# A layer's second product on one core: its operands split where they are made, and stored as two words

## The chip, the core and the metric

The kernel runs on one core of a Trainium2 chip. A core has TensorE (PE in the profile, with PEld for its weight loads), VectorE (DVE), ScalarE (ACT), GpSimd (POOL) and SyncE (SP), each with its own queue of instructions, which it works off in order and in which a semaphore wait holds everything behind it. SP issues most DMAs here, ACT and POOL issue some. The metric is the device time of one execution in microseconds (us), the median of several; lower is better.

## The reference, cut to what matters

```python
x1 = ln(alpha * x + (1 + g1) * (merged @ w_out), ...)   # 1024 rows of the prompt and 64 of the sample, 1024 wide
u2 = x1 * (1 + sc2) + sh2
f  = square(relu(u2 @ w_up + b_up)) @ w_down + b_down    # 1024 -> 4096 -> 1024
y  = ln(alpha * x1 + (1 + g2) * f, ...)
```

The first two thirds of the time go to the recurrent and attention branches that make `merged`; the change does not touch them. It touches the last third: the **up stage** (`u2 @ w_up`, bias, relu, square) and the **down stage** (`... @ w_down`).

## The kernel before

All products are done with three matmuls in place of one (`mm3`, lines 110 to 113): each float32 operand is split into a high word, rounded to the format that TensorE multiplies, and a low word, the rest. ACT writes the high word (a Copy), DVE subtracts it from the source for the low word. Line 111 is high by high, 112 and 113 are the cross terms. Weights are split after each load by `wsplit` (lines 91 to 99: raw tile `wr`, words `wh` and `wl`, three buffers of each) or `split` (101 to 108).

The 1088 tokens stand as columns in three groups: 0 and 1 of 384 columns, 2 of 320. The hidden width of 4096 is 32 blocks of 128, worked in 16 **pairs** of two blocks.

**The up stage.** Pairs 0 and 1 are computed beside the end of the layer before (`up_mm`, tiles `up` and `hr`), pairs 2 and 3 plainly (`up`, `c`), pairs 4 to 15 in groups 0 and 1 by Strassen's scheme: seven products of half size, into three PSUM tiles `xu`, `zu`, `yu`, in the order x, z, x with the sum T2, y with T1, x with T3, y, x with T4. Between them `after` copies and adds the products on ACT and DVE to the four results `c0` to `c3`; a product that adds to `xu` waits for the copy that reads `xu` (`c_0` from ACT before T2, `c_1` before T3). The sums T1 to T4 are built once from u2 (lines 700 to 722, tiles `tt`). Group 2 is plain: tiles `ug`, results `cg`. `put_pair` (630 to 641) then forms four further sums `t` on POOL from the pair's four results, and writes seven 128 by 384 tiles to the scratch tensor `hs_d` in device memory, three by DMAs of ACT's queue, four by POOL's; `put_g2` writes group 2's results to `hg_d`.

**The down stage.** Group 2's product for hidden blocks of the first half comes first: sixteen blocks of 24 matmuls (`dg`), by weights `wr_dg` and operands `hg`; its accumulator `fg` is loaded from `facc_d`, scaled, and added to. Then Strassen chunks 0 to 3 (tiles `xd`, `zd`, `yd`): each chunk needs seven operands `op` from `hs_d` and adds to `facc`. After them group 2's second half, and the last normalization. Each operand is loaded raw (tag `opr`, two buffers) and split by `op_split` into `oph` and `opl` (seven buffers each). The loads are issued by SP in one order. The last pair's group 2 (pair 15, `ug15`) is done on the way over, its result in `cgl`.

The order of instructions on each engine is set when the program is built, by a scheduler that follows the dependences; `tc.issue_after` puts an instruction behind another one.

## Time and profile before

| | |
|---|---|
| median of three runs | 1742.97 us (1742.93 to 1744.25) |
| the profiled execution: its own time | 1744.55 us |
| the profiled execution: its span | 1742.8 us |
| PE busy | 1703.7 us, 98% of the span |
| DVE, ACT, POOL busy | 1008.6, 779.9 and 403.3 us |
| DMA, mean over the span | 125 GB/s |

The span is the profiled time from the first to the last instruction; some 1.7 us of the execution's own time lie around it. Busy shares are averages over stages with different limits; where an engine stood idle, and which instruction of another engine ended the idle time, is to be read stage by stage.

### The profile page before, as it was taken

What the parts mean: (1) busy time and instruction counts of PE and PEld (TensorE: products, weight loads), DVE (VectorE), ACT (ScalarE), POOL (GpSimd) and SP (SyncE); (2) the same over time, 40 slices, a digit from 0 to 9 for tenths busy, and PEclk for the clock granted to TensorE, in tenths of its full rate; (3) what the DMA queues carried; (4) which work ended last, traced back from release to release, by engine and by line L of the source; (5) the groups of instructions that cost most, each with busy time, mean ns of one, the idle gap of its engine ahead of it and who ended that gap; (6) DMA issues with size and microseconds to landing.
All of it is one profiled execution on the core that took longest, in us unless ns stands there. A gap on an engine that the chain in (4) does not pass through costs nothing.

```text
span 1742.8 us, 26601 instructions
## 1 busy us (share of the span) xinstructions
PE 1703.7 (98%) x10632; PEld 1668.7 (96%) x10632; DVE 1008.6 (58%) x1605; ACT 779.9 (45%) x1169; POOL 403.3 (23%) x408
## 2 busy tenths in 40 slices
PE   7999999999999999999999999999999899999996
PEld 4999999999999999999999999999999799999996
DVE  4586553745537455374656758233332477898876
ACT  2452443625435253352634445455554753344343
POOL 1100010000100001000013233556664134443323
PEclk8999999999999999999999999999999999999999
DMA  9242312223131221212246633333333773454443
GB/s 355 96 131 70 102 51 71 75 70 102 51 105 53 75 84 57 99 55 70 63 137 206 194 120 128 129 127 127 127 128 129 284 280 116 171 185 148 159 167 108
DMA packets 88044, 218.08 MB, mean 125 GB/s; under 512 B 11504, under 2 KB 42480, under 8 KB 87920
## 3 DMA queue, kind: packets, MB, share of 16 engines
q1 hardware_dynamic: 71936, 188.46, 32.0%
q10 hardware_dynamic: 11888, 15.34, 2.5%
q0 software_dynamic: 4096, 12.59, 2.0%
q8 instruction: 83, 1.36, 0.3%
q14 instruction: 41, 0.34, 0.1%
HBM read 171.53 MB, written 44.83 MB: 124 GB/s over the span
## 4 chain that ended last, share of the span: by engine, by line
PE 91%; DVE 3%; DMA 2%; issue 2%; ACT 2%; POOL 0%; SPq 0%; DVEq 0%; ACTq 0%; POOLq 0%
PE z L113 13%; PE z L112 13%; PE z L111 13%; PE po L408 3%; PE s L397 2%; PE dg L111 2%; PE dg L113 2%; PE xd L111 2%; PE dg L112 2%; PE xd L113 2%; PE xd L112 2%; PE xu L111 2%; PE xu L112 2%; PE xu L113 2%; PE op L113 2%
## 5 line engine op out<-in xcount | busy, mean ns | idle before, releaser
L111 PE MATMUL z<-uh,wh_in 128*128 128x384 f32 (+1 forms) x1320 | 436.6, 331 | 2.9 <-ACT uh L103 2.9
L112 PE MATMUL z<-ul,wh_in 128*128 128x384 f32 (+1 forms) x1320 | 437.0, 331 | 0.8 <-DVE ul L104 0.8
L113 PE MATMUL z<-uh,wl_in 128*128 128x384 f32 (+1 forms) x1320 | 436.0, 330 | 0.0
L111 PEld LDWEIGHTS z<-uh,wh_in 128*128 128x128 f32 x1320 | 248.7, 188 | 6.3 <-ACT uh L103 3.9
L112 PEld LDWEIGHTS z<-ul,wh_in 128*128 128x128 f32 x1320 | 248.6, 188 | 4.9 <-DVE ul L104 2.8
L113 PEld LDWEIGHTS z<-uh,wl_in 128*128 128x128 f32 x1320 | 248.6, 188 | 4.0 <-issue 3.1
L97 ACT ACTIVATE wh_in<-wr_in 128x1024 fp32r<-128x1024 f32 x56 | 59.4, 1060 | 96.3 <-PE z L112 91.4
L98 DVE TENSOR_TENSOR wl_in<-wr_in,wh_in 128x1024 fp32r<-128x1024 f32 x56 | 68.4, 1221 | 40.3 <-ACT wh_in L97 40.3
L113 PE MATMUL dg<-ophg,wl_dg 128*128 128x320 f32 x256 | 79.8, 313 | 4.8 <-DVE wl_dg L98 4.8
L111 PE MATMUL dg<-ophg,wh_dg 128*128 128x320 f32 x256 | 80.8, 316 | 3.1 <-ACT wh_dg L97 3.1
L112 PE MATMUL dg<-oplg,wh_dg 128*128 128x320 f32 x256 | 79.7, 311 | 0.0
L161 DVE SCALAR_TENSOR_TENSOR ap<-ar,sil,ap 128x512 f32<-128x512 f32 x112 | 79.7, 743 | 0.0
L380 ACT ACTIVATE pr<-pr,st 128x640 f32<-128x640 f32 (+2 forms) x64 | 44.7, 698 | 57.6 <-DVE st L379 57.4
L457 POOL MEMSET er<- 128x1 f32 x8 | 1.1, 135 | 297.1 <-DVE rt L453 297.1
L104 DVE TENSOR_TENSOR slo_u<-sr_u,shi_u 128x1024 fp32r<-128x1024 f32 x24 | 31.3, 1305 | 64.9 <-ACT shi_u L103 64.9
L104 DVE TENSOR_TENSOR wlo_u<-wr_u,whi_u 128x1024 fp32r<-128x1024 f32 x24 | 34.7, 1447 | 56.7 <-ACT whi_u L103 56.7
L104 DVE TENSOR_TENSOR opl<-op,oph 128x1536 fp32r<-128x1536 f32 x28 | 59.8, 2136 | 12.9 <-ACT oph L103 12.8
L363 DVE COPY v<-vt 128x512 f32<-128x512 f32 x16 | 11.1, 691 | 97.0 <-PE vt L362 97.0
L103 ACT ACTIVATE shi_d<-sr_d 128x1024 fp32r<-128x1024 f32 x32 | 33.8, 1057 | 74.2 <-PE yd L112 56.5
L404 ACT ACTIVATE pts<-pt 128x512 f32<-128x512 f32 (+2 forms) x64 | 33.2, 519 | 74.5 <-PE pt L402 73.5
L408 PE MATMUL po<-pts,v 128*128 128x128 f32 x480 | 64.1, 275 | 0.5 <-ACT pts L404 0.3
L408 PEld LDWEIGHTS po<-pts,v 128*128 128x128 f32 x480 | 61.2, 191 | 1.2 <-ACT pts L404 1.2
(384 smaller groups left out, 4581.1 us busy)
## 6 DMA issues: line engine op xcount, KB each, us to landing
wr_in<-in_w_in SPq DMA_DIRECT2D x56, 512.0 KB, 3.3
ar<-in_w_ada SPq DMA_DIRECT2D x46, 512.0 KB, 4.9
op<-hs_d SPq DMA_DIRECT2D x28, 768.0 KB, 4.9
wr_u<-in_w_up SPq DMA_DIRECT2D x33, 512.0 KB, 3.6
wr_dg<-in_w_down SPq DMA_DIRECT2D x32, 512.0 KB, 4.3
wr_d<-in_w_down SPq DMA_DIRECT2D x32, 512.0 KB, 4.0
wr_o<-in_w_out SPq DMA_DIRECT2D x24, 512.0 KB, 3.5
hs_d<-t POOLq DMA_DIRECT2D x64, 192.0 KB, 2.9
```

Source lines behind the costliest of these rows:

```text
L97: hlast[0] = S.activation(hi, raw, AF.Copy).ins
L98: V.tensor_tensor(lo, raw, hi.bitcast(F32), op=ALU.subtract)
L103: first = S.activation(hi, src, AF.Copy).ins
L104: V.tensor_tensor(lo, src, hi.bitcast(F32), op=ALU.subtract)
L111: TE.matmul(ps, wh, xh, start=first, stop=False, skip_group_check=more)
L112: TE.matmul(ps, wh, xl, start=False, stop=False, skip_group_check=more)
L113: TE.matmul(ps, wl, xh, start=False, stop=last, skip_group_check=more)
L161: V.scalar_tensor_tensor(part[:, w, :], raw[:, j, :], sil[:, kb, w:w + 1], part[:, w, :], op0=ALU.mult, op1=ALU.add)
L380: S.activation(pr[:rows, :W], pr[:rows, :W], AF.Exp, bias=st[:rows, 0:1], scale=-1.0, accum_out=st[:rows, 1:2])
L397: TE.matmul(sps[:, bk, :cw], qq[:, q0:q0 + P], kk[:, P * j0 + c0:P * j0 + c0 + cw], start=(ip == 0), stop=(ip == 2))
L404: S.activation(pts[:, :min(W, 512)], pt[:, :min(W, 512)], AF.Copy)
L408: TE.matmul(po[:, :P], v[:, j0 + j, :], pts[:, P * j:P * j + P], start=(j == 0), stop=(j == nk - 1))
```

## The change

Every tile that goes to `hs_d` or `hg_d` is now split where it is made, and both words are written: `halves_of` has ACT copy the source into the first half of a new tile `o` (pair and number, `o14_3`; `og` for group 2) and DVE subtract into the second, and the DMA carries both, 384 KB in place of 192 KB. From pair 2 on, the `o` tiles share the three buffers of tag `tt`, of which each is free again when its DMA has landed. In the down stage `op_split` is gone: SP loads `hg` and `op` straight into operand tiles with both words (1280 KB and 1536 KB in place of half), all from one set of eight buffers. The first weight of the down stage is loaded ahead of `hg`. The 16 instructions that scale `fg` are GpSimd's (line 878 of the changed kernel) and no longer ACT's (867).

```diff
-        hs_d = dp.tile([NFF // 8, 7, P, 4, GW], F32, name="hs_d")
-        hg_d = dp.tile([P, NFF, TW2], F32, name="hg_d")
+        hs_d = dp.tile([NFF // 8, 7, P, 4, 2, GW], F32, name="hs_d")
+        hg_d = dp.tile([P, NFF, 2, TW2], F32, name="hg_d")
...
+        onew = [lambda nm: big([P, 2, GW], nm)]
+
+        def new_o(nm):
+            return onew[0](nm)
+
+        def halves_of(src, nm, o=None):
+
+            if o is None:
+                o = new_o(nm)[:, :, 0:src.shape[-1]]
+            S.activation(o[:, 0, :].bitcast(R32), src, AF.Copy)
+            V.tensor_tensor(o[:, 1, :], src, o[:, 0, :], op=ALU.subtract)
+            return o
+
         def put_pair(p, c11, c12, c21, c22, g2s, new_t):
...
             for k, src in enumerate((c11, c21, t2, t1, t3, c22, t4)):
-                (S if k in (0, 1, 5) else G).dma_start(hs_d[c, k][:, i, :], src)
+                (S if k in (0, 1, 5) else G).dma_start(hs_d[c, k][:, i, :, :], halves_of(src, f"o{p}_{k}"))
...
-        def put_g2(p, b, src):
+        def put_g2(p, b, src, o=None):
             c, i = divmod(p, 4)
-            S.dma_start(hg_d[:, 8 * c + 4 * b + i, :], src)
+            S.dma_start(hg_d[:, 8 * c + 4 * b + i, :, :], halves_of(src, f"og{p}_{b}", o))
...
+        onew[0] = lambda nm: fp.tile([P, 2, GW], F32, tag="tt", bufs=3, name=nm)
+
         def up_g2(p, wa, wb):
...
-                c = cgs[b] if p == LATE else fp.tile([P, TW2], F32, tag="cg", bufs=2, name=f"cg{p}_{b}")
+                if p == LATE and b > 0:
+                    cgs.append(hp.tile([P, 2, TW2], F32, tag="cg", name=f"cgl{b}"))
+                c = cgs[b][:, 1, :] if p == LATE else fp.tile([P, TW2], F32, tag="cg", bufs=2, name=f"cg{p}_{b}")
                 relu2(c, ps[:, :TW2], f)
-                put_g2(p, b, c)
+                put_g2(p, b, c, cgs[b] if p == LATE else None)
...
-        cgs = [hp.tile([P, TW2], F32, tag="cg", bufs=2, name=f"cgl{b}") for b in range(2)]
+        cgs = [hp.tile([P, 2, TW2], F32, tag="cg", name="cgl0")]
         facc = {fb: new_facc(fb) for fb in range(4)}
-        hi_ins = []
-
-        def op_split(src, nm):
-            hl = [hp.tile(list(src.shape), R32, tag=t, bufs=7, name=f"{t}{nm}") for t in ("oph", "opl")]
-            hi_ins.append(split(*hl, src))
-            return hl
 
         def load_hg(c, h):
-            o = hp.tile([P, 4, TW2], F32, tag="opr", bufs=2, name=f"hg{c}_{h}")
-            loads.append(SY.dma_start(o, hg_d[:, 8 * c + 4 * h:8 * c + 4 * h + 4, :]).ins)
-            return op_split(o, f"g{c}_{h}")
+            o = hp.tile([P, 4, 2, TW2], R32, tag="op", bufs=8, name=f"hg{c}_{h}")
+            loads.append(SY.dma_start(o.bitcast(F32), hg_d[:, 8 * c + 4 * h:8 * c + 4 * h + 4, :, :]).ins)
+            return o[:, :, 0, :], o[:, :, 1, :]
...
-                                    S.activation(fg[:, fb, c0:c1], fg[:, fb, c0:c1], AF.Identity, scale=sA[:, fb:fb + 1],
-                                                 bias=bA[:, fb, w:w + 1])
+                                    G.tensor_scalar(fg[:, fb, c0:c1], fg[:, fb, c0:c1], sA[:, fb:fb + 1], bA[:, fb, w:w + 1],
+                                                    op0=ALU.mult, op1=ALU.add)
...
-        hg = {(0, h): load_hg(0, h) for h in range(2)}
-        with tc.issue_after(loads[1]):
-            pre = [wsplit(a["w_down"][0, 0], "dg0_0_0")]
-        with tc.issue_after(hi_ins[0]), tc.issue_after(hlast[0]):
+        pre = [wsplit(a["w_down"][0, 0], "dg0_0_0")]
+        with tc.issue_after(wlast[0]):
+            hg = {(0, h): load_hg(0, h) for h in range(2)}
+        with tc.issue_after(hlast[0]):
             up_g2(LATE, *wt)
...
-                o = hp.tile([P, 4, GW], F32, tag="opr", bufs=2, name=f"op{c}_{k}")
+                o = hp.tile([P, 4, 2, GW], R32, tag="op", bufs=8, name=f"op{c}_{k}")
                 with tc.issue_after(wloads[-1] if c == 0 and k > 4 else loads[-1]):
-                    loads.append(SY.dma_start(o, hs_d[c, k]).ins)
-                ops.append(op_split(o, f"{c}_{k}"))
+                    loads.append(SY.dma_start(o.bitcast(F32), hs_d[c, k]).ins)
+                ops.append((o[:, :, 0, :], o[:, :, 1, :]))
```

The built programs differ in order at three places that matter below. First DVE, where pairs 0 and 1 end (`uf`, `u2h`, `u2l`: the last columns of u2; `wl_u2` is the low word of pair 2's weights). Before:

```order
L586 TENSOR_SCALAR uf2_256_9692<-nT2_256_9690,s2_8188,b2_8189 128x64 x8
L104 TENSOR_TENSOR u2l2_9360<-uf2_256_9692,u2h2_9359 128x8x64
L98 TENSOR_TENSOR wl_u0_9815<-wr_u0_9812,wh_u0_9814 128x1024
L705 TENSOR_TENSOR tt0_0_9888<-u2h0_8527,u2l0_8528 128x768
L705 TENSOR_TENSOR tt0_1_9889<-u2h1_8939,u2l1_8940 128x768
L705 TENSOR_TENSOR tt0_2_9890<-u2h1_8939,u2l1_8940 128x768
L713 TENSOR_TENSOR tt0_0_9888<-tt0_1_9889,tt0_0_9888 128x768
L98 TENSOR_TENSOR wl_u2_9941<-wr_u2_9938,wh_u2_9940 128x1024
L98 TENSOR_TENSOR wl_u6_9947<-wr_u6_9944,wh_u6_9946 128x1024
```

and in the changed program, from the middle of pair 1's subtractions on (line 640; the subtractions of `o0_0` to `o0_3` stand ahead of `u2l`, the rest of pair 0 and `o1_0`, `o1_1` after it):

```order
L640 TENSOR_TENSOR o1_2_9905<-t1_1_9890,o1_2_9905 128x384
L640 TENSOR_TENSOR o1_3_9909<-t1_0_9889,o1_3_9909 128x384
L640 TENSOR_TENSOR o1_4_9913<-t1_2_9891,o1_4_9913 128x384
L640 TENSOR_TENSOR o1_5_9917<-hr5_9626,o1_5_9917 128x384
L640 TENSOR_TENSOR o1_6_9921<-t1_3_9892,o1_6_9921 128x384
L640 TENSOR_TENSOR og1_0_9925<-hr1_9523,og1_0_9925 128x320
L640 TENSOR_TENSOR og1_1_9929<-hr5_9626,og1_1_9929 128x320
L718 TENSOR_TENSOR tt0_0_9942<-u2h0_8527,u2l0_8528 128x768
L718 TENSOR_TENSOR tt0_1_9943<-u2h1_8939,u2l1_8940 128x768
L718 TENSOR_TENSOR tt0_2_9944<-u2h1_8939,u2l1_8940 128x768
L726 TENSOR_TENSOR tt0_0_9942<-tt0_1_9943,tt0_0_9942 128x768
L98 TENSOR_TENSOR wl_u2_9995<-wr_u2_9992,wh_u2_9994 128x1024
```

All of pairs 0 and 1 now stands ahead of the three joins, the subtraction and `wl_u2`; ACT's copies for them stand in the same order on ACT, the last nine (`o1_0` to `o1_6`, `og1`) and those of `og0` behind the square of `hr0`.

Second ACT, between pair 14 and pair 15 (lines 617 and 618 are relu and square; 802 and 807 of the kernel before are 819 and 824 of the changed one). Before:

```order
L618 ACTIVATE c14_2_12370<-c14_2_12370 128x384
L618 ACTIVATE cg14_1_12568<-cg14_1_12568 128x320
L639 DMA hs_d_87<-c14_2_12370 128x384
L645 DMA hg_d_88<-cg14_1_12568 128x320
L802 ACTIVATE c15_0_12572<-xu15_12602 128x384
L617 ACTIVATE c15_0_12572<-c15_0_12572,bup_78 128x384
L618 ACTIVATE c15_0_12572<-c15_0_12572 128x384
L639 DMA hs_d_87<-c15_0_12572 128x384
L807 ACTIVATE c15_1_12573<-xu15_12602 128x384
L809 ACTIVATE c15_3_12575<-yu15_12604 128x384
```

and now:

```order
L617 ACTIVATE c14_2_12748<-xu14_12776,bup_78 128x384
L618 ACTIVATE c14_2_12748<-c14_2_12748 128x384
L639 ACTIVATE o14_1_12889<-c14_2_12748 128x384
L639 ACTIVATE o14_2_12893<-t14_1_12878 128x384
L639 ACTIVATE o14_3_12897<-t14_0_12877 128x384
L819 ACTIVATE c15_0_12977<-xu15_13007 128x384
L652 DMA hs_d_87<-o14_1_12889 128x768
L617 ACTIVATE c15_0_12977<-c15_0_12977,bup_78 128x384
L618 ACTIVATE c15_0_12977<-c15_0_12977 128x384
L639 ACTIVATE o14_4_12901<-t14_2_12879 128x384
L639 ACTIVATE o14_5_12905<-c14_3_12749 128x384
L824 ACTIVATE c15_1_12978<-xu15_13007 128x384
```

Five copies (line 639) and other instructions stand between pair 14's last square and `c15_1`; `o14_4` waits for the landing of `o14_1`'s DMA and `o14_5` for that of `o14_2`'s, whose buffers they take. On PE in the changed program pair 15's x, z and y with T1 stand ahead of pair 14's last product, so that T2, T3 and T4 of pair 15 follow pair 14's T4 with no other matmul but pair 15's y between them; before, x, z and y of pair 15 stood between.

Third SP, at the start of the down stage (each row is one DMA). Before:

```order
L848 DMA hg1_0_12842<-hg_d_88 128x1280
L848 DMA hg1_1_12848<-hg_d_88 128x1280
L863 DMA fg_12807<-facc_d_86 128x8x320
L93 DMA wr_dg0_0_3_12909<-in_w_down 128x1024
L93 DMA wr_dg0_1_0_12939<-in_w_down 128x1024
L93 DMA wr_dg0_1_1_12987<-in_w_down 128x1024
L897 DMA op0_0_13361<-hs_d_87 128x1536
L905 DMA facc0_12729<-facc_d_86 128x768
L905 DMA facc1_12730<-facc_d_86 128x768
L897 DMA op0_1_13367<-hs_d_87 128x1536
L93 DMA wr_dg0_1_2_13019<-in_w_down 128x1024
L93 DMA wr_dg0_1_3_13051<-in_w_down 128x1024
```

and now, the same stretch, from the third `hg` on:

```order
L859 DMA hg1_0_13264<-hg_d_88 128x2560
L859 DMA hg1_1_13266<-hg_d_88 128x2560
L874 DMA fg_13229<-facc_d_86 128x8x320
L93 DMA wr_dg0_0_2_13293<-in_w_down 128x1024
L93 DMA wr_dg0_0_3_13323<-in_w_down 128x1024
L908 DMA op0_0_13775<-hs_d_87 128x3072
L908 DMA op0_1_13777<-hs_d_87 128x3072
L908 DMA op0_2_13779<-hs_d_87 128x3072
L908 DMA op0_3_13781<-hs_d_87 128x3072
L916 DMA facc0_13154<-facc_d_86 128x768
L916 DMA facc1_13155<-facc_d_86 128x768
L93 DMA wr_dg0_1_0_13353<-in_w_down 128x1024
```

Four whole `op` tiles and two `facc` now stand ahead of `wr_dg0_1_0`, the weights of the fifth of the sixteen blocks `dg`, where one row `op` stood behind three of the rows `wr_dg`.

## Rows read from the trace of the kernel before

**Rows 1.** The page: the chain that ended last, by engine.
```profile
PE 91%; DVE 3%; DMA 2%; issue 2%; ACT 2%; POOL 0%; SPq 0%; DVEq 0%; ACTq 0%; POOLq 0%
```

**Rows 2.** Timeline of PE, 1036 to 1056 us: start, length, instruction, [idle before].
```profile
1037.57 0.71 PE L111 MATMUL up<-u2h,wh_u 128*128 128x320 f32 x3 [1.68 <-ACT u2h L103]
...
1054.72 0.34 PE L113 MATMUL up<-u2h,wl_u 128*128 128x384 f32 x1
```

**Rows 3.** Timeline of DVE, 1036 to 1049 us.
```profile
1037.55 0.69 DVE L104 TENSOR_TENSOR u2l<-uf,u2h 128x512 fp32r<-128x512 f32 x1 [0.70 <-ACT u2h L103]
...
1044.06 2.69 DVE L705 TENSOR_TENSOR tt<-u2h,u2l 128x768 f32<-128x768 f32 x3
...
1047.54 1.22 DVE L98 TENSOR_TENSOR wl_u<-wr_u,wh_u 128x1024 fp32r<-128x1024 f32 x1
```

**Rows 4.** Timeline of ACT, 1034 to 1056 us (ACTq: a DMA issue).
```profile
1053.60 0.47 ACT L618 ACTIVATE hr<-hr 128x320 f32<-128x320 f32 x1
1054.10 0.33 ACTq L645 DMA_DIRECT2D hg_d<-hr  x1
```

**Rows 5.** ACT's groups by form, 1100 to 1350 us: busy us, mean ns, idle before.
```profile
L618 ACT ACTIVATE c<-c 128x384 f32<-128x384 f32 x45 | 23.6, 524 | 1.1
...
L617 ACT ACTIVATE c<-c,bup 128x384 f32<-128x384 f32 x35 | 21.4, 612 | 50.8 <-DVE c L811 31.9 <-DVE c L804 18.9
...
L807 ACT ACTIVATE c<-xu 128x384 f32<-128x384 f32 x12 | 5.7, 472 | 2.4 <-DMA hg<-hg_d 2.4
```

**Rows 6.** One of DVE's groups by form, 1100 to 1350 us.
```profile
L811 DVE TENSOR_TENSOR c<-xu,c 128x384 f32<-128x384 f32 x12 | 6.7, 557 | 23.4 <-PE xu L113 23.4
```

**Rows 7.** Two of POOL's groups by form, 1100 to 1350 us.
```profile
L639 POOL DMA_DIRECT2D hs_d<-t x47 | 25.8, 551 | 0.0
...
L637 POOL TENSOR_TENSOR t<-c,t 128x384 f32<-128x384 f32 x12 | 12.3, 1027 | 0.2
```

**Rows 8.** DMA issues, 1200 to 1300 us: KB each, median us from issue to landing.
```profile
wr_u<-in_w_up SPq DMA_DIRECT2D x10, 512.0 KB, 3.5
hs_d<-t POOLq DMA_DIRECT2D x17, 192.0 KB, 3.4
hs_d<-c ACTq DMA_DIRECT2D x14, 192.0 KB, 1.9
```

**Rows 9.** Stretches: length, busy (count) of PE, PEld, DVE, ACT, POOL, clock, DMA share, GB/s.
```profile
1170.00:1191.30 21.30, 21.30 (x131) 21.30 (x131) 7.06 (x7) 11.11 (x20) 12.56 (x13) 1.00 0.37 126
1366.00:1368.00 2.00, 2.00 (x9) 2.00 (x9) 2.00 (x3) 0.00 (x0) 0.00 (x0) 0.50 0.86 323
1370.00:1380.00 10.00, 7.46 (x51) 7.20 (x50) 1.38 (x1) 7.49 (x17) 0.00 (x0) 1.00 1.04 421
1480.00:1500.00 20.00, 19.33 (x111) 19.01 (x111) 17.33 (x16) 10.43 (x10) 9.03 (x4) 1.00 0.56 199
1500.00:1520.00 20.00, 20.00 (x117) 19.86 (x116) 15.62 (x20) 5.29 (x6) 10.37 (x8) 1.00 0.43 165
1600.00:1620.00 20.00, 18.76 (x106) 17.93 (x105) 17.55 (x17) 10.38 (x9) 7.56 (x4) 1.00 0.73 249
```

**Rows 10.** Timeline of PE at the first matmul of pair 15's T3.
```profile
1346.74 0.44 PE L111 MATMUL xu<-T3h,shi_u 128*128 128x384 f32 x1 [0.63 <-ACT c L807]
```

**Rows 11.** Timeline of PE from the end of the up stage to the first chunk.
```profile
1353.12 0.31 PE L111 MATMUL ug<-u2h,whi_u 128*128 128x320 f32 x1
...
1360.15 0.31 PE L111 MATMUL dg<-ophg,wh_dg 128*128 128x320 f32 x1
...
1365.39 0.58 PE L113 MATMUL dg<-ophg,wl_dg 128*128 128x320 f32 x1 [4.78 <-DVE wl_dg L98]
...
1380.21 0.42 PE L111 MATMUL dg<-ophg,wh_dg 128*128 128x320 f32 x1 [2.75 <-ACT wh_dg L97]
...
1426.74 0.34 PE L111 MATMUL xd<-oph,whi_d 128*128 128x384 f32 x1
```

**Rows 12.** DMA issues, 1366 to 1376 us.
```profile
wr_dg<-in_w_down SPq DMA_DIRECT2D x2, 512.0 KB, 8.7
```

More of the change, by code (lines that the diff above doesn't have):

```diff
@@ L951, in final2_open @@
                     TE.transpose(pt[:cw, P * fb:P * fb + P], fg[:, fb, c:c + cw], ident)
-                y = hp.tile([P, D], F32, tag="shi" if c < 2 * P else "opl", bufs=2 if c < 2 * P else 7, name=f"y2_{c}")
+                y = hp.tile([P, D], F32, tag="shi" if c < 2 * P else "op", bufs=2 if c < 2 * P else 8, name=f"y2_{c}")
                 S.activation(y[:cw, halves[0]], pt[:cw, :], AF.Copy)
```

## The prediction

> **What bounds the kernel now.** I read the chain that ended last first: 91% of it is PE [rows 1], so time is gained or lost only where PE waits. Then the stretches of the last third. A stretch as long as one pair of the up stage shows PE busy without a gap, with ACT at 11.1 of 21.3 us and DVE at 7.1 [rows 9]: both have room, if what they do comes in time. Last the few places where PE stands idle: 1.68 us before the last columns of u2 [rows 2], 0.63 us in pair 15 [rows 10], and the start of the down stage [rows 11]. There 48 matmuls `ug` take 7.03 us from 1353.12 to 1360.15, so 0.1465 each; the sixteen blocks `dg` of 24 should take 56.3 us, and the first chunk should begin at 1416.4. It begins at 1426.74: 10.3 us are lost, 4.78 and 2.75 of them in two waits, the rest in short ones and in a clock that stood at 0.50 behind the first [rows 9]. At that clock 13 matmuls cost about 1.6 us more than at the full one; behind the 2.75 us the clock was 1.00. In the chunks a stretch holds 117 matmuls where nothing is lost, and 111 to 106 in the three in which a chunk gives way to the next [rows 9].
>
> **Pairs 0 and 1.** The change adds, for each pair, nine copies on ACT and nine subtractions on DVE. A copy is as `c_1`'s, 0.47 us; a subtraction as line 811's, 0.56 us [rows 5, 6]; DMA issues are 0.33 us on ACT [rows 4]. What counts is where they stand. Four subtractions stand ahead of `u2l`'s last part, for which PE waits within a microsecond [rows 2, 3]: 2.2 us less the 0.7 us that DVE idles there, **+1.5 us**. Then, as the order shows, eleven copies and four DMA issues follow the square of `hr0`, which ends at 1054.07 [rows 4]: 11 x 0.47 + 4 x 0.33 = 6.5, to 1060.6. DVE's last subtraction ends at 1061.2; only then come the joins and the subtraction that before ran from 1044.06 to 1047.54, 3.5 us, and `wl_u2`, 1.22 us [rows 3]: 1065.9. PE uses `wl_u2` at 1054.72 [rows 2], with nothing else to do, as its queue holds the matmuls in order. **+11.2 us**, and +1.6 for the clock, since a wait of 4.78 us was enough to halve it. The later sums T then have the time that PE was given: nothing.
>
> **Steady pairs.** ACT gets 4.2 us and DVE 5.0 us per pair, which fits the room above. But a tile `o` takes one of three buffers, free when its DMA has landed. A tile of 384 KB was not timed; 192 KB took 1.9 us from ACT's queue and 3.4 from POOL's, 512 KB 3.5 from SP's [rows 8]. I take 2.5 and 3.5, nearer to the small ones, since most of a landing does not grow with size between these rows. Nine tiles in three rounds of some 5 us fit the pair of 21.3 us. In pairs 4 to 13 the scheduler has the next pair's products as filler before T3; by the same reckoning as below `c_1` is there at about the same time as PE, and I take **+2 us** for ten pairs (0 to 5). POOL's added waits before its next weight sums are covered by a whole pair.
>
> **Pairs 14 and 15.** There the filler ends. Pair 14: T3 follows T2 by two matmuls, and ACT's `c14_1` stands behind three copies of pair 13, of which the first waits for a DMA issued some 3 us earlier: **+2.6 us**. Pair 15, counted from A, the end of pair 14's T4: relu 0.6, square 0.5, three copies 1.4, `c15_0` 0.5 [rows 5]: T2 starts at A+3.0 and not at A. `o14_1`'s DMA is issued at A+3.3 and lands at A+5.8; `o14_2`'s is issued on POOL behind `t14_3` (1.03) and 0.55 of issue [rows 7], and lands at A+6.4; two copies, then `c15_1` at A+7.4, where T2 was done at A+5.1. T3 and y take 4.1 us, to A+11.5; the addition on DVE that T4 needs stands behind `og14_1`, whose buffer chain ends in the landing of `o14_4` at A+11.1, so A+13.1. Lost 3.0 + 2.3 + 1.6 = 6.9, before 0.63 [rows 10]: **+6.3 us**.
>
> **The start of the down stage.** Let E be the end of pair 15's T4 (before, 1353.12). Gained: no splits of `hg`, and GpSimd scales `fg`, so that ACT is free for `wh_dg`, which 2.75 us were lost to. Lost: the weights. In the order of SP's queue, what is still to be moved from about E+4 until `wr_dg0_1_0` has landed is three `hg` (3.9 MB), `fg` 1.3, four `wr_dg` 2.1, four `op` 6.3, two `facc` 0.8: 14.4 MB. The engines of the DMAs were full (share 1.04) at 421 GB/s [rows 9]; at 0.41 MB a us that is 35 us. A weight load in such a stretch landed 8.7 us after its issue, against 3.5 in the calm [rows 8, 12]: transfers queued on SP come behind those queued before. So the weight lands at E+39 + 2 = E+41 if pair 15's written tiles (3.3 MB, in other queues) are gone by then, and at E+49 if they take their full share: I take E+44.5, and 2.3 us for the two words. PE needs it after `ug` and four blocks, 7.0 + 14.1 = E+21.1, so it will have lost 25.7 us, before it 10.3: **+15.4 us** (12 to 20), and +1 for a clock that falls again. What follows comes 1.3 us apart, faster than PE's 3.5 us blocks.
>
> The Trainium skill, "DMA: Bandwidth & Descriptors" (Specifications), gives about 358 GB/s as what device memory yields to one core; by it, 14.4 MB would take 40 us, and this term would be 5 us more. The trace's 421 GB/s disagrees, and the trace decides.
>
> **The chunks.** ACT and DVE lose 28 splits of `op`; PE lost 6 matmuls of 20/117 = 0.171 us at the first of the three transitions and 11 at the last, 1.0 and 1.9 us, so 4 to 5 us in all. Eight buffers are free one after the other, a load of 1.5 MB takes 4 us, and PE needs them about 4 us apart: I take **-4 us** (0 to -5).
>
> **The sum.** 1.5 + 11.2 + 1.6 + 2 + 2.6 + 6.3 + 15.4 + 1 - 4 = +37.6. The profiled execution took 1744.55 us, 1.6 above the median of the runs: 1744.55 + 37.6 - 1.6 = 1780.5, **1780 us**.
>
> **Rivals.**
> Weights overtake: if SP's transfers share the engines and do not queue, `wr_dg0_1_0` lands some 10 us after its issue and PE waits there as before or less: without the 16.4 us, 1764 us. For it: transfers were spread over 16 engines; against it [rows 12].
> The Trainium skill, "DMA: Bandwidth & Descriptors" (Queues, rings and completion order), says that completion is not first-in first-out for one issuing engine, though descriptors start in ring order; that speaks for a part of this rival. The landing of 8.7 us [rows 12] disagrees with it where one queue is full, and so the rival has 0.14 and no more.
> ACT bounds the steady pairs: if a landing takes 5 us and not 2.5 to 3.5, `c_1` comes 2 us late in ten pairs, +18 more: 1798 us. It decides from a landing of about 4 us; [rows 8] speak against it for ACT's queue, less for POOL's.
> Faster: DVE reaches `wl_u2` before 1054.72, because the copies of pairs 0 and 1 fall into idle time of ACT, and with every operand ready as it lands the down stage loses nothing. Then -10.3 - 4.5 + 1.5 + 8.9 + 2 = -2.4, and with half of the two last pairs' waits -6.9: 1736 us. It decides at the start of the joins, which must be before 1050. Against it stands the built order, with eleven copies behind the square of `hr0`.
> No change: the losses above halve and the gains come in full: 1744 us.
>
> **Chances.** Forecast 0.60 (1768 to 1794), weights overtake 0.14, ACT bound 0.12, faster 0.09, no change 0.05. What a measurement can tell from no change is about 0.2%, 3.5 us. Range 1757 to 1802: it takes in both rivals beside the forecast and leaves out the last two and the tails. Faster 0.09, same 0.05, slower 0.86.
>
> **What would show it.** PE waiting some 11 us for DVE's `wl_u` at line 98, near 1056 us; PE waiting for ACT's `c` (lines 819, 824) twice at the end of the up stage; PE waiting for `wh_dg` or `wl_dg`, whose ACT or DVE waits for a `wr_dg`, for 10 to 15 us at once before the fifth `dg`; 117 matmuls in every 20 us of the chunks. The prediction is wrong if DVE's joins start before 1055, or if a `wr_dg` issued behind the four `op` lands in less than 10 us, or if PE shows waits inside pairs 4 to 13.

## The result and the profile after

The changed kernel takes 1809.03 us (median of four runs, 1808.47 to 1811.3), the kernel before 1742.95: a ratio of 1.0376, 95% interval 1.0364 to 1.0388. It is slower by 66 us where 37 were forecast, and outside the range (1757 to 1802). The profiled execution took 1809.23 us, with a span of 1807.4 from its first to its last instruction; before, the span was 1742.8.

The waits of PE in the changed kernel (us in total, times, longest). Lines 819, 824 and 828 were 802, 807 and 811: the copies to `c_0` and `c_1` and the addition for which the next product of a pair waits.

```profile
PE dg L111 <- ACT wh_dg L97: 17.7, 3, 8.2
PE up L113 <- DVE wl_u L98: 10.6, 1, 10.6
PE yu L111 <- ACT shi_u L103: 9.4, 4, 3.2
PE xu L111 <- ACT c L819: 8.8, 8, 3.8
PE xu L111 <- ACT c L824: 6.1, 5, 1.9
...
PE dg L111 <- DMA hg<-hg_d: 4.1, 1, 4.1
...
PE xu L111 <- DVE c L828: 2.0, 2, 1.4
```

The third to fifth row and the last lie inside pairs 4 to 15; before, there was one such wait there, 0.63 us [rows 10]. The largest of them, 9.4 us, is for `shi_u`, the high word of a sum of weights, which ACT also copies in its order behind the tiles `o`. The chain that ended last shows the same, against 91% PE before [rows 1]:

```profile
PE 75%; DMA 6%; DVE 5%; POOL 5%; issue 4%; ACT 4%; SPq 0%; ACTq 0%; DVEq 0%; POOLq 0%
```

Where the time went is read from the starts of four rows of PE's timeline: pair 2's weight, the first matmul of pair 4's second product (`zu`), the first `ug` behind pair 15, and the first matmul of the first chunk.

```profile
1063.26 0.69 PE L113 MATMUL up<-u2h,wl_u 128*128 128x384 f32 x1 [10.59 <-DVE wl_u L98]
...
1111.62 0.33 PE L111 MATMUL zu<-u2h,whi_u 128*128 128x384 f32 x1
...
1400.92 0.31 PE L111 MATMUL ug<-u2h,whi_u 128*128 128x320 f32 x1
...
1496.14 0.34 PE L111 MATMUL xd<-op,whi_d 128*128 128x384 f32 x1
```

Before, `zu` came at 1101.54, `ug` at 1353.12 and `xd` at 1426.74 [rows 11]. So four stretches carry the whole difference of the spans:

| stretch | before, us | after, us | difference | predicted |
|---|---|---|---|---|
| start, to `zu` of pair 4 | 1101.5 | 1111.6 | +10.1 | +14.3 |
| pairs 4 to 15, `zu` to `ug` | 251.6 | 289.3 | +37.7 | +10.9 |
| down start, `ug` to `xd` | 73.6 | 95.2 | +21.6 | +16.4 |
| chunks, `xd` to the end | 316.1 | 311.3 | -4.8 | -4 |
| sum | 1742.8 | 1807.4 | +64.6 | +37.6 |

Stretches of the changed kernel, with the columns of [rows 9]. The clock is TensorE's granted clock as a share of full speed, the DMA share the busy share of the DMA engines. The first is 244 us of pairs, with PE idle for 18.3 of them and 1331 matmuls. The next three are the down start: clock 0.72 and DMA share 1.03 where the waits stand. The last two are chunks, 117 matmuls each; every 20 us from 1500 to 1720 hold 117 or 118, where before the transitions between chunks had 111 to 106.

```profile
1109.00:1353.00 244.00, 225.69 (x1331) 220.61 (x1330) 152.08 (x159) 148.43 (x278) 132.33 (x119) 0.99 0.52 186
...
1404.00:1424.00 20.00, 13.82 (x70) 12.76 (x69) 5.44 (x7) 4.00 (x8) 3.76 (x6) 0.76 0.93 349
1424.00:1444.00 20.00, 11.19 (x57) 10.26 (x55) 2.99 (x3) 3.47 (x5) 9.29 (x16) 0.72 1.03 424
1444.00:1464.00 20.00, 11.98 (x69) 11.58 (x70) 7.48 (x9) 7.30 (x7) 0.00 (x0) 0.83 0.69 257
1500.00:1520.00 20.00, 20.00 (x117) 20.00 (x116) 13.63 (x17) 9.14 (x10) 11.83 (x8) 1.00 0.67 267
...
1620.00:1640.00 20.00, 20.00 (x117) 20.00 (x116) 10.89 (x14) 4.76 (x5) 6.92 (x5) 1.00 0.68 272
```

What happens where PE waits in a pair shows from 1142 to 1151 us, all engines but PE. The tiles `o` here are pair 4's; pair 5 runs on PE.

```profile
1142.02 0.51 ACT L639 ACTIVATE o<-t 128x384 fp32r<-128x384 f32 x1
...
1142.48 1.33 POOL L650 TENSOR_TENSOR t<-c,t 128x384 f32<-128x384 f32 x1
1142.88 1.35 DVE L640 TENSOR_TENSOR o<-t,o 128x384 f32<-128x384 f32 x1
1143.76 0.56 POOL L652 DMA_DIRECT2D hs_d<-o  x1
...
1144.53 0.54 POOL L652 DMA_DIRECT2D hs_d<-o  x1 [0.20 <-issue]
...
1146.43 0.53 ACT L639 ACTIVATE o<-c 128x384 fp32r<-128x384 f32 x1
...
1146.99 0.56 DVE L640 TENSOR_TENSOR o<-c,o 128x384 f32<-128x384 f32 x1
...
1149.95 0.52 ACT L639 ACTIVATE o<-t 128x384 fp32r<-128x384 f32 x1 [2.99 <-DMA hs_d<-o]
1149.97 0.33 ACTq L652 DMA_DIRECT2D hs_d<-o  x1
1150.38 0.47 ACT L824 ACTIVATE c<-xu 128x384 f32<-128x384 f32 x1
```

And PE:

```profile
1150.90 0.44 PE L111 MATMUL xu<-T3h,shi_u 128*128 128x384 f32 x1 [1.94 <-ACT c L824]
```

The copy at 1149.95 is that of the pair's seventh tile, and it waits for the buffer of the fourth. That one was copied at 1142.02, subtracted until 1144.23, issued on GpSimd at 1144.53, and landed some 5.4 us later: a round of 7.9 us. This is a long one. Over pairs 4 to 15 a round took 5.4 us on the average (the mean landing less the mean start of the copies, 106 tiles), 3.2 of them the landing, and of the three buffers two were taken on the average. Behind the waiting copy stand, in ACT's order, two things. One is the issue of the sixth tile's DMA (1149.97), whose subtraction had ended at 1147.55, so the next round starts 2.4 us late. The other is `c5_1` (line 824), for which PE waits 1.94 us until 1150.90. From pair 4 to 15 ACT stands still for landings of these tiles 33 times, 31.6 us in all.

At the down start ACT has the same kind of row. Timeline of SP, then of ACT:

```profile
1425.10 2.07 SPq L908 DMA_DIRECT2D op<-hs_d  x4
1427.22 2.49 SPq L916 DMA_DIRECT2D facc<-facc_d  x2
1430.74 5.20 SPq L93 DMA_DIRECT2D wr_dg<-in_w_down  x2
```

```profile
1448.28 2.01 ACT L918 ACTIVATE facc<-facc,bA,sA 128x768 f32<-128x768 f32 x2 [13.91 <-DMA facc<-facc_d]
1450.56 1.06 ACT L97 ACTIVATE wh_dg<-wr_dg 128x1024 fp32r<-128x1024 f32 x1 [0.27 <-DMA wr_dg<-in_w_down]
```

The weight of the fifth block is issued behind four `op` tiles and two `facc` (it is the first of the two of 1430.74), and is there about 20 us later, 49.6 us after the first `ug`; ahead of it ACT scales `facc`, which had to land first. From 4 us after the first `ug` until that landing the DMA engines have no slack:

```profile
1404.90:1450.50 45.60, 24.11 (x118) 22.12 (x117) 7.54 (x9) 9.46 (x14) 12.15 (x21) 0.76 0.99 393
```

At a share of 0.99 they move 17.9 MB, 15.1 of them SP's and 2.8 the last tiles of pair 15, which ACT and GpSimd store. SP stands 14.8 us for the landing of the last of these, from 1408.9 to 1423.8 us, but the engines stay full meanwhile (1.00), so that wait alone delays nothing.

### The profile page after: what moved, and what is told of

Its sections match the earlier page's. It is cut to its first block, busy times and chain, and to the rows that moved or that the text cites. A ratio compares the mean times of both kernels' runs of the same rounds, so it can differ in the third digit from the quotient of the medians.

```text
span 1807.4 us, 26784 instructions
## 1 busy us (share of the span) xinstructions
PE 1720.4 (95%) x10632; PEld 1681.2 (93%) x10632; DVE 1058.3 (59%) x1713; ACT 783.8 (43%) x1261; POOL 423.6 (23%) x424
## 4 chain that ended last, share of the span: by engine, by line
PE 75%; DMA 6%; DVE 5%; POOL 5%; issue 4%; ACT 4%; SPq 0%; ACTq 0%; DVEq 0%; POOLq 0%
PE z L113 12%; PE z L112 12%; PE z L111 12%; DMA hs_d<-o 4%; PE po L408 3%; PE xd L113 2%; PE xd L111 2%; PE xd L112 2%; PE s L397 2%; PE dg L113 2%; PE dg L111 2%; PE dg L112 2%; PE op L113 2%; PE op L112 2%; PE op L111 2%
## 5 line engine op out<-in xcount | busy, mean ns | idle before, releaser
L111 PE MATMUL dg<-hg,wh_dg 128*128 128x320 f32 x256 | 83.5, 326 | 21.8 <-ACT wh_dg L97 17.7
L97 ACT ACTIVATE wh_in<-wr_in 128x1024 fp32r<-128x1024 f32 x56 | 59.4, 1060 | 96.3 <-PE z L112 91.4
L113 PE MATMUL dg<-hg,wl_dg 128*128 128x320 f32 x256 | 82.3, 321 | 1.2 <-DVE wl_dg L98 1.2
L112 PE MATMUL dg<-hg,wh_dg 128*128 128x320 f32 x256 | 82.1, 321 | 0.0
L640 DVE TENSOR_TENSOR o<-t,o 128x384 f32<-128x384 f32 x64 | 49.8, 798 | 48.1 <-ACT o L639 48.1
L111 PEld LDWEIGHTS dg<-hg,wh_dg 128*128 128x128 f32 x256 | 50.7, 198 | 23.0 <-ACT wh_dg L97 18.7
L98 DVE TENSOR_TENSOR wl_dg<-wr_dg,wh_dg 128x1024 fp32r<-128x1024 f32 x32 | 40.7, 1274 | 39.2 <-ACT wh_dg L97 38.8
L113 PE MATMUL up<-u2h,wl_u 128*128 128x384 f32 (+1 forms) x160 | 52.9, 335 | 10.6 <-DVE wl_u L98 10.6
## 6 DMA issues: line engine op xcount, KB each, us to landing
op<-hs_d SPq DMA_DIRECT2D x28, 1536.0 KB, 11.6
```

The source lines that it names most:

```text
L97: hlast[0] = S.activation(hi, raw, AF.Copy).ins
L98: V.tensor_tensor(lo, raw, hi.bitcast(F32), op=ALU.subtract)
L111: TE.matmul(ps, wh, xh, start=first, stop=False, skip_group_check=more)
L112: TE.matmul(ps, wh, xl, start=False, stop=False, skip_group_check=more)
L113: TE.matmul(ps, wl, xh, start=False, stop=last, skip_group_check=more)
L640: V.tensor_tensor(o[:, 1, :], src, o[:, 0, :], op=ALU.subtract)
```

## The experiments

Times in us; the stretches are those of the table above, from one profiled execution each. "Pairs" is what is over the 251.6 us of before, "start" what is over 1101.5. In the two runs with pair 2's weights first, two matmuls of `zu` stand ahead of pair 3's last ones, and the boundary is the third. The profiled execution lies within 3 us of the median, but 5.2 above it for the six plain buffers. The kernel before ran beside each group at 1742.98 to 1744.02.

| run | time | start | pairs | down start | chunks |
|---|---|---|---|---|---|
| before | 1742.95 | 0 | 0 | 73.6 | 316.1 |
| changed | 1809.03 | 10.1 | 37.7 | 95.2 | 311.3 |
| nine buffers | 1783.82 | 13.1 | 7.9 | 96.5 | 311.3 |
| no words | 1759.85 | -1.0 | 0.0 | 94.4 | 311.3 |
| no subtraction | 1785.26 | 6.0 | 20.6 | 94.1 | 311.3 |
| no words, pairs 0, 1 | 1798.29 | -1.0 | 39.4 | 96.3 | 311.3 |
| op loads later | 1800.43 | 11.4 | 35.4 | 83.6 | 315.1 |
| fg on ACT | 1809.69 | 11.3 | 36.9 | 96.1 | 311.4 |
| weights of pair 2 first | 1807.26 | 3.6 | 38.9 | 97.0 | 311.3 |
| six buffers, in place | 1796.43 | 13.2 | 22.2 | 94.7 | 311.3 |
| six plain buffers | 1793.97 | 14.2 | 22.3 | 96.4 | 311.3 |
| loads in order of need | 1797.79 | 10.0 | 36.2 | 80.2 | 316.9 |
| before, fg on GpSimd | 1740.18 | 0.3 | 0.0 | 70.1 | 317.5 |
| before, words of hg only | 1744.90 | 1.8 | -0.3 | 71.9 | 316.7 |
| o issued on SP | 1800.90 | 9.7 | 25.7 | 97.6 | 311.4 |
| six, SP, op later | 1778.66 | 13.7 | 4.8 | 86.8 | 316.8 |

**Nine buffers.**
```diff
-        tag="tt", bufs=3
+        tag="tt", bufs=9
...
+        tl = fp.tile([P, 4, GW], R32, tag="tl", name="Tl")
-            ut[k] = (..., fp.tile([P, 4, GW], R32, tag=f"t{k}l", name=f"T{k}l"))
+            ut[k] = (..., tl)
```


> Nine buffers for the two-word tiles in place of three, in the space of three sums T's low words (T2, T3 and T4 write their low words over T1's, so the results are slightly off; the instructions and their number stay). What is asked: what makes pairs 2 to 15 take 37.7 us longer than before. Theory buffers: ACT stands in order before a copy until one of three tiles has landed, and the copies c, whi and shi that PE needs stand behind it. Then the first ug of pair 15 comes some 25 to 30 us earlier than 1400.9 and the time is 1779 to 1786. Theory work: the copies and subtractions themselves delay ACT and DVE, wherever the buffers stand; then 1803 to 1809. Theory traffic: twice the bytes make each landing and the weight loads late; then 1806 to 1809.


Measured: 1783.82. The pairs lose 7.9 us, all of it behind 1353 us, at pair 15 (waits of 3.58 and 0.58 us, and a clock of 0.76 from 1353 to 1374); until then PE has no gap, as before. The start loses 3 us more than with three buffers, and 3 to 4 in all runs with six; PE's wait for `wl_u` is 13.2 us here, and why was not followed. Its stretch of 244 us against the changed kernel's above, and what a landing took in it from 1110 to 1350 us:

```profile
1109.00:1353.00 244.00, 244.00 (x1489) 244.00 (x1489) 146.23 (x176) 163.91 (x308) 137.31 (x128) 1.00 0.56 201
```
```profile
hs_d<-o POOLq DMA_DIRECT2D x44, 384.0 KB, 4.1
hs_d<-o ACTq DMA_DIRECT2D x34, 384.0 KB, 4.3
```
PE issues 158 matmuls more. ACT is busier (163.9 us against 148.4) and never stands for a landing, and landings are longer than in the changed kernel, where they took 2.9 and 3.0 there. So it is neither ACT's work nor the landing by itself. With a buffer always free, ACT's rows show how the tiles of a pair come:

```profile
1137.44 0.53 ACT L639 ACTIVATE o<-t 128x384 fp32r<-128x384 f32 x1 [0.97 <-POOL t L648]
1137.87 0.51 ACT L639 ACTIVATE o<-t 128x384 fp32r<-128x384 f32 x1
...
1138.74 0.53 ACT L639 ACTIVATE o<-t 128x384 fp32r<-128x384 f32 x1
1139.17 0.51 ACT L639 ACTIVATE o<-c 128x384 fp32r<-128x384 f32 x1
1140.03 0.53 ACT L639 ACTIVATE o<-t 128x384 fp32r<-128x384 f32 x1 [0.35 <-POOL t L650]
1140.46 0.81 ACT L639 ACTIVATE og<-cg 128x320 fp32r<-128x320 f32 x2
```

Seven of the nine are copied within 4 us, and a round of them took 7.2 us on the average here. So seven to nine buffers are taken at once in each pair, and none in 29% of the time: with fewer, some copy of the burst has to wait.

**No words.** The stored tiles are the source, twice; no copy and no subtraction.
```diff
-            S.activation(o[:, 0, :].bitcast(R32), src, AF.Copy)
-            V.tensor_tensor(o[:, 1, :], src, o[:, 0, :], op=ALU.subtract)
-            return o
+            return src.unsqueeze(1).to_broadcast([P, 2, src.shape[-1]])
```


> No copy and no subtraction for the stored words; each tile is written from its source to both planes, so the DMAs move the same bytes and the low words in memory are not low words. Theories buffers and work agree: the waits of pairs 2 to 15 go (37.7 us) and the wait for wl_u at the start too (10 us): 1758 to 1766, with the first ug of pair 15 within 3 us of where it stood before the change, 1353.1. Theory traffic: only the 10 us at the start go, 1796 to 1800.


Measured: 1759.85. Twice the bytes written cost the pairs nothing. The down start keeps its 94.4 us: what it loses is in the loads, not in the splits.

**No subtraction.**
```diff
-            V.tensor_tensor(o[:, 1, :], src, o[:, 0, :], op=ALU.subtract)
-            return o
+            return o[:, 0:1, :].to_broadcast([P, 2, src.shape[-1]])
```


> The copy to the high word stays, with its three buffers; the subtraction on DVE is left out and the high word is written to both planes. Theory buffers: the copy still waits for landings, only the DVE time of 0.5 to 2.2 us drops out of each tile's round, so a half of the 37.7 us at most: 1785 to 1797 with what the start gives back (some 5 us). Theory work, if it is DVE's work beside GpSimd's: nearly all of it, 1764 to 1772.


Measured: 1785.26, at the edge of the first theory's span and outside the second's. The pairs still lose 20.6 us, ACT still stands for landings (42 us in 36 waits), so leaving the subtraction out gives back 17 of the 37.7. A round is shorter by 0.6 us then (4.8 against 5.4); DVE and GpSimd have less to do as well, and the two were not separated.

**No words in pairs 0 and 1.**
```diff
+            def twice(src):
+                return src.unsqueeze(1).to_broadcast([P, 2, src.shape[-1]])
+
...
-                (...).dma_start(hs_d[c, k][:, i, :, :], halves_of(src, f"o{p}_{k}"))
+                (...).dma_start(hs_d[c, k][:, i, :, :], twice(src) if p < 2 else halves_of(src, f"o{p}_{k}"))
...
-                put_g2(p, b, src)
+                S.dma_start(hg_d[:, 8 * c + 4 * b + i, :, :], twice(src))
```


> Copies and subtractions are left out for pairs 0 and 1 alone, whose sources are written to both planes; pairs 2 to 15 as in the changed kernel. If the 10.6 us in which PE stands for wl_u at 1063 us are the queue of these copies on ACT and subtractions on DVE, the wait goes and the time is 1797 to 1800; if later waits take it up, 1803 to 1809.


Measured: 1798.29. The wait for `wl_u` is gone; the start term is these copies and subtractions.

**Op loads later.**
```diff
-                with tc.issue_after(wloads[-1] if c == 0 and k > 4 else loads[-1]):
+                with tc.issue_after(wloads[-1] if c == 0 and k > 4 else wdg[(8, 10, 12, 14, 15)[k]] if c == 0 else loads[-1]):
```


> The first five loads of op are issued behind the 9th, 11th, 13th, 15th and 16th of the sixteen weight loads wr_dg instead of ahead of the fifth; with them the loads and scalings of facc go back. From the first ug of pair 15 to the first chunk the changed kernel takes 95.2 us, the kernel before 73.6, and the matmuls alone 63.3. Theory order (a weight lands behind the op tiles queued before it): the waits of 7.8 and 8.2 us for wh_dg shrink to below 3 together, and the low clock behind them goes: 67 to 78 us in this stretch, 1782 to 1792. Theory bytes (the stretch moves more than the DMA engines can bring, in any order): 88 us or more, 1802 to 1809.


Measured: 1800.43, between the theories. The stretch from `ug` to `xd` shortens by 11.6 us, one of the two long waits goes, the other stays at 6.84. And 3.8 us are lost again in the chunks, most of them in the first: 105 matmuls from 1484 to 1504 us and 108 in the next 20, where PE waits twice for `wlo_d`, 3.1 us in all.

**Fg on ACT.**
```diff
-                                    G.tensor_scalar(fg[:, fb, c0:c1], fg[:, fb, c0:c1], sA[:, fb:fb + 1], ...)
+                                    S.activation(fg[:, fb, c0:c1], fg[:, fb, c0:c1], AF.Identity, ...)
```


> One part undone: ACT scales fg again, as before the change, everything else as changed. My step said that GpSimd's scaling frees ACT for wh_dg. If the weights' landing is what wh_dg waits for, it makes no difference: 1806 to 1812. If ACT's sixteen scalings, which have to wait for fg's landing, stand ahead of weights that are there: 1813 to 1820.


Measured: 1809.69, no difference, which agrees with the first case: in the changed kernel `wh_dg` waits for the weights whichever engine scales.

**Weights of pair 2 first.**
```diff
+        w2 = [up_w(f) for f in fblocks(2)]
         for p in range(2):
             h1, h2 = (hraw[f] for f in fblocks(p))
```


> The two weights of pair 2 are loaded and split ahead of the copies of pairs 0 and 1 in the program, no longer behind the first sum of T; the joins and sums T follow pair 1's copies. Theory order at the start: PE's wait of 10.6 us for wl_u goes: 1797 to 1801. Rival: the sums T come so late that PE waits for them at pair 4, or the copies of pairs 2 and 3 pile up behind them: 1804 to 1812.


Measured: 1807.26, the rival's side. The wait shrinks from 10.59 to 4.34 us and pair 4 starts 6.5 us earlier, but the pairs and the down start take back 3.0, and the profiled execution gains only 3.4. Why these two stretches grew was not followed further.

**Six buffers, in place.** `t` and `cg` are made in the second plane of their tile.
```diff
-            t1, t2, t3, t4 = (new_t(f"t{p}_{k}") for k in range(4))
+            to = {k: new_o(f"o{p}_{k}") if p > 1 else None for k in (3, 2, 4, 6)}
+            t1, t2, t3, t4 = (new_t(f"t{p}_{k}") if o is None else o[:, 1, :] for k, o in to.items())
...
-        tag="tt", bufs=3
+        tag="tt", bufs=6
-        tag="c", bufs=9
+        tag="c", bufs=6
```


> Six buffers with every word right: the tiles t and cg are made in the second plane of their two-word tile and the subtraction works in place, so nine tiles c become six and three more two-word tiles fit. t and cg then hold a tile from their making on, and c has two spare tiles where it had one for c and t together. Theory buffers: pairs 2 to 15 lose 10 to 20 us instead of 37.7: 1781 to 1793. If six with longer holding are as few as three: 1800 to 1812.


Measured: 1796.43; the pairs lose 22.2, a little more than expected.

**Six plain buffers.** The nine-buffer edit with a six.


> As the run with nine buffers, with six (the sums T2 to T4 again write their low words over T1's, so the results are slightly off). Nine tiles a pair, and a tile is held for copy, subtraction, issue and landing alone. Theory buffers, by their number: between nine and three, nearer to nine: the twelve pairs 4 to 15 lose 8 to 16 us and not 37.7 (nine: 7.9); 1783 to 1792. If what counts is that all nine tiles of a pair fit at once, six lose over 20 us: above 1796.


Measured: 1793.97, between the two cases. In the profiled execution the pairs lose 22.3 and not 8 to 16, but it took 1799.19, so that up to 5 of them may be its own. The run before lost 22.2 in an execution at its median: with three, six and nine buffers 37.7, some 22 and 7.9, about 5 us for each buffer. Holding the tiles longer for `t` and `cg` cost at most the 2.5 us between the two medians. A round took 6.8 and 7.4 us in these two runs, so that fewer than three of the six buffers are taken on the average; still ACT stands 23.0 and 20.5 us for landings, as the burst wants more than six.

**Loads in order of need.** As the op loads later, and:
```diff
-                        if b == 1 and (c + 1, 0) not in hg and c + 1 in cs:
+                        if b == 3 and (c + 1, 0) not in hg and c + 1 in cs:
```


> As the run with the op loads behind the weights; besides, the second two loads of hg and the load of fg are issued behind the fourth weight load instead of behind the second. What the stretch loads is the same. In the run before, PE still stood 6.8 us for the third weight, which lay behind 3.9 MB of hg and fg. Theory order: that wait shrinks below 3 us and the stretch from the first ug of pair 15 to the first chunk goes from 83.6 us to 74 to 79: 1791 to 1796. Theory bytes: PE waits as long for hg instead, 1798 to 1802.


Measured: 1797.79, between the two. The wait for the weight falls from 6.84 to 4.38 us and the stretch from 83.6 to 80.2; the chunks lose 1.8 more. With both edits order is worth 15 us of the stretch, and about a third of it is lost again in the chunks.

**Before, with fg on GpSimd.** The kernel before with one part of the change.


> One part of the change alone, on the kernel before: GpSimd scales fg. Before, ACT scales fg for 6.7 us at 1372.5, after 2.65 us of waiting for its landing, and PE stands 2.75 us for the wh_dg behind it, with a low clock after. My step on the down start: these 2.75 us and 1 to 2 us of clock come back: 1738 to 1741. Rival: another wait of the stretch (hg's split, a weight's landing) takes its place: 1742 to 1744.


Measured: 1740.18 against 1743.65 beside it, a ratio of 0.998 (0.9971 to 0.9989): a small gain, clear of the noise, and the fastest kernel of the study. PE's waits from 1340 to 1440 us, here and then in the kernel before:

```profile
PE dg L113 <- DVE wl_dg L98: 5.0, 1, 5.0
PE xu L111 <- ACT c L807: 0.6, 1, 0.6
```
```profile
PE dg L113 <- DVE wl_dg L98: 4.8, 1, 4.8
PE dg L111 <- ACT wh_dg L97: 3.1, 2, 2.7
PE xu L111 <- ACT c L807: 0.6, 1, 0.6
```
The waits for `wh_dg` are gone, nothing in the stretch takes their place, and it is 3.5 us shorter. The profiled execution loses 1.4 of them again in the chunks, where PE waits 1.6 us for `wlo_d` (before 0.4); it took 1742.77, the longest of its eleven runs.

**Before, with words of hg only**: two words for `hg`, GpSimd for `fg`, pair 2's weights first, loads in order of need.
```diff
-            o = hp.tile([P, 4, TW2], F32, tag="opr", bufs=2, name=f"hg{c}_{h}")
-            loads.append(SY.dma_start(o, hg_d[:, 8 * c + 4 * h:8 * c + 4 * h + 4, :]).ins)
-            return op_split(o, f"g{c}_{h}")
+            hl = [hp.tile([P, 4, TW2], R32, tag=t, bufs=7, name=f"{t}g{c}_{h}") for t in ("oph", "opl")]
+            for j in range(2):
+                ld = SY.dma_start(hl[j].bitcast(F32), hg_d[:, 8 * c + 4 * h:8 * c + 4 * h + 4, j, :]).ins
...
```


> The kernel before with the parts that the runs speak for: only the 320-column operand hg is stored as two words (two tiles of a pair, not nine, pass the three buffers), hs stays one word and is split as before; GpSimd scales fg; pair 2's weights are split ahead of the copies of pairs 0 and 1; loads at the down start stand in order of need. Theory buffers and order: pairs as before the change within 3 us, and the down start loses 2 to 6 us instead of 10.3: 1736 to 1742. Rival: words of og, however few, make ACT wait for landings in the pairs, or two words of hg make the stretch wait for bytes: 1746 to 1755.


Measured: 1744.90, 1.0007 (0.9999 to 1.0016): no difference from the kernel before, and 4.7 us more than with `fg` on GpSimd alone. With two tiles a pair instead of nine, the three buffers cost the pairs nothing (-0.3). The down start is 1.8 us longer than in the run above: PE stands 5.91 us for one `wh_dg`, where the other stood 4.98 for `wl_dg`. The three further parts gain nothing together; which of them costs the 4.7 us was not separated.

**O issued on SP.**
```diff
-                (S if k in (0, 1, 5) else G).dma_start(hs_d[c, k][:, i, :, :], ...)
+                (SY if p > 1 else S if k in (0, 1, 5) else G).dma_start(hs_d[c, k][:, i, :, :], ...)
...
-            S.dma_start(hg_d[:, 8 * c + 4 * b + i, :, :], ...)
+            (SY if p > 1 else S).dma_start(hg_d[:, 8 * c + 4 * b + i, :, :], ...)
```


> Three buffers, the same copies, subtractions and bytes; the nine DMAs of a pair from 2 on are issued on SP instead of ACT and GpSimd. At 1149.97 us of the changed kernel an issue on ACT stood 2.4 us behind a copy that itself waited for another tile's landing, so a buffer's round holds a wait in ACT's queue beside copy, subtraction and landing. If that is a large part of it, pairs 4 to 15 lose 18 to 28 us and not 37.7: 1793 to 1802. If the round is landing and subtraction, and the copies behind them in ACT's order are the whole of it: 33 to 40, 1805 to 1812. Weights loaded on SP behind these issues could come late: then above 1812.


Measured: 1800.90. The pairs lose 25.7: 12 of the 37.7 us are the issue's place in ACT's and GpSimd's queues. Landings from 1110 to 1350 us are not shorter (3.3 us in the median for `hs_d`).

**Six buffers, SP, op loads later.** The three edits together.


> Every word right: six buffers with t and cg made in place, issues on SP, op loads behind the weights. If the three work on different waits their gains add: 12.6 (six buffers) and 8.6 (op loads) give 1788, and what SP's issue gives is taken off. If SP's queue holds the weight loads up instead: above 1790.


Measured: 1778.66. The single gains are 12.6, 8.1 and 8.6, together 29.3; the run gains 30.4. The totals add, but the stretches do not: the pairs give back 32.9, where the two edits alone gave 15.5 and 12.0, and the down start 8.4 instead of 11.6. So it is not shown that each edit works on a wait of its own. The pairs then lose 4.8 us.

## Why the prediction was wrong

**The step that failed** is the one on the steady pairs: "Nine tiles in three rounds of some 5 us fit the pair of 21.3 us", and so +2 for ten pairs. From 1109 to 1353 us, pairs 4 to 13 and the beginning of 14, PE falls 158 matmuls behind the run with nine buffers, some 26 us where 2 stood, and stands idle 17 times: the prediction's own sign of being wrong, waits inside pairs 4 to 13.
The size of the round was right. It was 5.4 us on the average (landings 2.9 us from ACT's queue and 3.1 from GpSimd's in the median, assumed 2.5 and 3.5), and three rounds are 16 us of a pair that took 24. What was wrong is the step from a fit on the average to no wait. The nine tiles do not come evenly: seven are copied within 4 us where no buffer is missing, and seven to nine buffers are taken at once. With three, ACT stood 33 times before a copy until a tile had landed, and the copies that PE needs (`c_0`, `c_1`, `shi`) stand behind it in ACT's order. With nine buffers ACT's waits for landings and PE's waits before 1353 us are gone, although landings are longer.
Two terms were priced too low besides. The subtraction was priced at 0.56 us; its mean is 0.80, since it often runs beside GpSimd's sums. Leaving it out gave back 17 us. The issue was priced at 0.33 us on ACT, and not as an instruction that stands in order behind a copy which waits. Moving it gave back 12 us. The two were not taken away together, so it is not shown that these gains add.
The general idea was on record at pair 15, where the same wait of a copy ahead of `c_1` was reckoned out; for the other ten pairs the scheduler's filler was trusted to cover it.

**The rival that ACT bounds the pairs** named the right place and a wrong point of decision: landings of over 4 us. With nine buffers they took 4.1 and 4.3 and PE lost nothing in those pairs; with three they took 3 and it lost some 26.

**Pairs 14 and 15**, 8.9 us, came near in size, in part by luck. Behind 1353 us the changed kernel lost 12.2. PE's waits in pair 15 for the `c_0` and the `c_1` copy came, 3.75 and 1.80 us (predicted 3.0 and 2.3). The waits in pair 14 for `c_1` (2.6) and in pair 15 for DVE's addition (1.6) did not; instead there was one of 2.56 for `shi_u`, and 4.1 us went at a low clock and in the first matmuls behind the waits, which were not priced:

```profile
1374.84 0.45 PE L111 MATMUL yu<-T1h,shi_u 128*128 128x384 f32 x1 [2.56 <-ACT shi_u L103]
...
1387.25 0.69 PE L111 MATMUL xu<-T2h,shi_u 128*128 128x384 f32 x1 [3.75 <-ACT c L819]
...
1392.97 0.45 PE L111 MATMUL xu<-T3h,shi_u 128*128 128x384 f32 x1 [1.80 <-ACT c L824]
```

With nine buffers 7.9 remain, so most of this is not the buffers'.

**Pairs 0 and 1** were right in mechanism: PE waits 10.59 us for `wl_u` (predicted 11.2), and it goes with these copies. The +1.5 for `u2l` did not come: PE waits 1.11 us for it where it waited 1.68 for `u2h`. The start came out 4.2 us under its sum.

**The down start** was right in mechanism and 5 us short. Weights do come behind the `op` tiles: the fifth landed 49.6 us after the first `ug` (predicted 44.5), and moving the `op` loads back shortens the stretch by 11.6. The sum had 41 us without the tiles that pair 15 still writes and 49 with them, and took a value between; the tiles took their full share, 2.8 of the 17.9 MB that kept the DMA engines full. So the term that was mis-sized is these bytes. The low clock is not it: PE stood for the fifth weight until 1451.67 us, and behind that the stretch loses 2.3 us, where 1 was priced. The rival that weights overtake is out: the sixteen DMAs that SP issued from 1406 to 1441 us landed in the order of their issue. The 8.7 us of [rows 12] alone, one landing time, did not yet show this order. The Trainium skill, "DMA: Bandwidth & Descriptors" (Specifications), gives about 358 GB/s as a core's share of the memory; from 1424 to 1444 us the trace shows 424, so that page's figure did not bound this stretch. The 5 us more that it would have given come out near the measured time by luck.

**The fg scaling** was right for the kernel before (3.5 us) and is hidden in the changed one (0.7 us, within the spread of the runs), where ACT would wait for the weights anyway. **The chunks** gave 4.8 us for 4, the same in every kernel whose `op` loads were not moved.

## What to carry to other kernels

A buffer's round is everything from the first write to the landing, the waits in two or three in-order queues included. That tiles over buffers times the round is less than the period doesn't show that nothing waits: here it was 16 of 24 us with three buffers and some 10 of 23 with six, and the pairs lost 37.7 and 22. Ask how many tiles are held at once when nothing waits (here seven to nine), and what stands in order behind the instruction that waits for a buffer. Work moved from a late stage to an earlier one isn't free because the engines there have idle time: here 144 small splits took the place of 36 large ones, in front of the copies that PE waits for. When several parts are changed at once, the smallest can be the one worth keeping: scaling `fg` on GpSimd alone is 0.2% faster than the kernel before.

## What was not expected of the hardware

A subtraction of 128x384 on DVE that takes 0.56 us alone took up to 2.18 beside GpSimd. The longest, from the timeline of the changed kernel:

```profile
1127.62 0.54 POOL L652 DMA_DIRECT2D hs_d<-o  x1 [0.22 <-issue]
1127.72 2.18 DVE L640 TENSOR_TENSOR o<-c,o 128x384 f32<-128x384 f32 x1 [0.40 <-ACT o L639]
1128.17 1.30 POOL L756 TENSOR_TENSOR sr_u<-sr_u,wr_u 128x512 f32<-128x512 f32 x1
```

It is longer by 1.62 us, GpSimd's sum beside it takes 1.30. Of the 112 such subtractions the 67 with no GpSimd sum beside them took 0.54 to 0.56 us, the other 45 took 1.17 on the average. The Trainium skill, "SBUF — State Buffer" (SBUF: two separate sides), says that a DVE instruction with two inputs in SBUF and a GpSimd one that reads SBUF hold one port pair in turn, the first for its whole length. All but one of the 45 agree with it: the 38 that began while a sum was running took 0.61 to 1.64 us, and of the seven that began before the sum six took 0.55 to 0.56. The row above is the exception, which began first and is the longest; spans on GpSimd are rough, and no run shows why.

Second, landings of the same 384 KB went from 2.9 and 3.0 us with three buffers to 4.1 and 4.3 with nine (GpSimd's queue and ACT's), at a DMA share of 0.56 against 0.52.
